# One decoder layer on one core: the first 256-column product behind 512-column products, done as two of 128 columns

## Chip, core and metric

The kernel runs on one core of a Trainium2 chip. The metric is the device time of one launch, in microseconds (us). TensorE is called PE (its weight loads PEld), VectorE DVE, ScalarE ACT, GpSimd POOL, and SyncE, which issues the weight DMAs, SP.

## What is computed

One layer on 256 tokens of width 2048: a half-step SwiGLU feed-forward (FFN), a mixer of sparse attention and a recurrent branch, and a second FFN, each followed by a layer norm. Nearly all of the arithmetic is in matrix products with weights that are read once.

```python
def swiglu(h, w_in, w_out):
    a, b = jnp.split(h @ w_in, 2, axis=-1)
    return (jax.nn.silu(a) * b) @ w_out

h = layer_norm(DN_ALPHA * h + 0.5 * swiglu(h, ffn1_w_in[l], ffn1_w_out[l]), ln1_g[l], ln1_b[l])
q, k, v, qi, ki, wi, rx, rg, gates = split_cols(h @ w_in[l])
...
y_attn = dsa_attention(q, k, v, qi, ki, wi)
y_rnn = rglru_branch(rx, rg, conv_w[l], conv_b[l], lru_wa[l], lru_ba[l], lru_wx[l], lru_bx[l], lru_lambda[l])
merged = g_attn * (y_attn @ w_attn_branch[l]) + g_rnn * (y_rnn @ w_rnn_branch[l])
h = layer_norm(DN_ALPHA * h + merged @ w_out[l], ln2_g[l], ln2_b[l])
h = layer_norm(DN_ALPHA * h + 0.5 * swiglu(h, ffn2_w_in[l], ffn2_w_out[l]), ln3_g[l], ln3_b[l])
```

## The kernel before

**Precision.** Every operand is split into two fp32r parts, a high half h and the rest l (ACT copies h, line 275; DVE subtracts to get l, line 276; the tile is `hl`). A product of two operands is three PE products: x_h·w_h, x_h·w_l, x_l·w_h. `three` (lines 743 to 745) issues these. The stationary operand is the activation (128 tokens), the moving one is the weight, and each product has its own weight load on PEld, also where two in a row have the same stationary operand.

**Two widths.** A weight piece is used either plainly, in products of 512 columns, once for each half of the tokens (`tokens`; pieces "c" of an input matrix and "o" of the FFN's output matrix), or in one of four *forms*, p1q3, p2, q5p7 and q4p6. The forms are a seven-product scheme for a 2x2 block of tokens and columns; their products have 256 columns. p2 has one operand, that is six products, and the others two, that is twelve. `blockF` runs a list of pieces (a plan), and its inner function `run` issues the products of a form. In the FFNs' main blocks (blocks 6 to 21 of 22) a plan holds 16 forms (four chunks of four) with four fills "o" among them, three ahead of the forms and one in the middle; in the other projections one or two chunks of forms alternate with plain pieces, or all are plain.

**What the forms cost elsewhere.** A form's weights are sums of weight blocks. For a chunk, DVE makes the sum tile `ws` (line 230, S below), the l part for p1q3 (`hl<-rf`), a further sum (line 234, A), the l part for p2, another sum in place (line 237, B), the l part for q5p7 (`hl<-ws`) and the l part for q4p6 (`hl<-rf`). ACT makes an h part ahead of each l part. A plain piece needs one h and one l part (`hl<-raw`), or none on DVE where its l part comes by an adding DMA (`wd`).

**Order.** PE, SP and POOL run in the order in which the program is written. DVE and ACT are ordered by the framework's scheduler, from the times that it assumes for all engines' instructions. `Weights.unit` loads and splits pieces some four ahead of PE; the ring of `hl` tiles holds five. At the end of an FFN block, `gate` combines the forms' results on DVE and ACT (tile `z`), and some pieces later PE transposes the result (four 128-column products) for the output matrix.

Of the kernel before, what the change touches and what calls it, by code (L numbers as in the profile page):

```python
# [16 lines left out]
S = 256  # L17
# [350 lines left out]
def tile_layer(ctx, tc, x_fm, x_tm, pos, f1a, f1o, wA, wki, wB, wG, lru, wab, wrb, wo, f2a, f2o,  # L368
# [6 lines left out]
    V, A, T, G = nc.vector, nc.scalar, nc.tensor, nc.gpsimd  # L375
    count = [0]

    def name(s):
        count[0] += 1
        return f"{s}{count[0]}"  # L380

    def U(s="u", dt=F32):
        return pool.tile([P, 512], dt, name=name(s), tag="u", bufs=U_BUFS)

    def UHL(s):
        return U(s, F32R).rearrange("p (a t) -> p a t", a=2)
# [10 lines left out]
    def MM():  # L397
        return psum.tile([P, 512], F32, name=name("mm"), tag="mm", bufs=4)

    def BP():  # L400
        return psum.tile([P, 512], F32, name=name("bp"), tag="bp", bufs=4)
# [60 lines left out]
    for i in range(NR + LAG):  # L462
# [4 lines left out]
        if i >= LAG:  # L467
            g, c = divmod(i - LAG, TPG)
# [17 lines left out]
    W = Weights(nc, pool, pieces, bg.paced)  # L486
# [6 lines left out]
    def share(which):  # L493

        shared.close()
        p = shared.enter_context(tc.tile_pool(name=name(which), bufs=1))
        lane[0] = p if which == "t" else None
        W.third = p if which == "s" else None
# [243 lines left out]
    def three(ps, xh, xl, w, start, stop):  # L742
        T.matmul(ps, xh, w[0], start=start, stop=False)  # L743
        T.matmul(ps, xh, w[1], start=False, stop=False)  # L744
        T.matmul(ps, xl, w[0], start=False, stop=stop)  # L745

    def tokens(ps, x, t, w, start, stop):
        three(ps, x[:, 0, t * P:(t + 1) * P], x[:, 1, t * P:(t + 1) * P], w, start, stop)

    def eager(hs, ps):  # L750
# [28 lines left out]
    def blockF(x, forms, plan, fill):  # L779

        c = e = None
        first, last = {}, {}
        for i, (f, k) in enumerate(plan):
            for b in BANKS.get(f, ()):
                first.setdefault(b, i)
                last[b] = i
        skip = 0
        if getattr(x, "halves", None):  # L790
            c = [MM(), MM()]
            eager(x, c)
            skip = 4
        for i, (form, k) in enumerate(plan):
            if i < skip:
                continue
            if form == "o":
                fill()
                continue
            if not c:  # L800
                c = [MM(), MM()]
            start, stop = ([f.get(b) == i for b in range(4)] for f in (first, last))
            if form == "c":
                for j in (k, k + 1):
                    w = W.unit(512)
                    for t in range(2):
                        tokens(c[t], x[j], t, w, start[t] and j == k, stop[t] and j > k)
                continue
            if not e:
                e = [BP(), BP()]  # L810
            c11, c12, c21 = c[0][:, :S], c[0][:, S:], c[1][:, :S]
            p1, p6, p7, q5 = e[0][:, :S], e[0][:, S:], e[1][:, :S], e[1][:, S:]
            fs = [forms[2 * k + r] for r in range(2)]

            def xop(i, t):
                return [tuple(x[4 * k + 2 * r + i][:, a, t * P:(t + 1) * P] for a in range(2)) for r in range(2)]

            def sop(i):
                return [tuple(v[:, i * P:(i + 1) * P] for v in fs[r]) for r in range(2)]

            def run(ps, ops, start, stop):
                for r in range(2):
                    three(ps, *ops[r], W.unit(S), start and r == 0, stop and r == 1)

            if form == "p1q3":
                run(p1, xop(0, 0), start[2], stop[2])
                run(c12, sop(3), start[0], stop[0])
            elif form == "p2":
                run(c11, xop(1, 0), start[0], stop[0])
            elif form == "q5p7":  # L830
                run(q5, sop(0), start[3], False)
                run(p7, sop(2), False, stop[3])
            else:
                run(c21, xop(1, 1), start[1], stop[1])
                run(p6, sop(1), start[2], stop[2])
        return c, e

    def blockA(x, finish=None, lag=0, ln=None):
# [6 lines left out]
        def half(t, k, w):  # L845
            tokens(ps[t], x[k], t, w, k == 0, k == n - 1)
# [30 lines left out]
    def split(dst, f):  # L877
        split.last = A.activation(dst[:, 0], f, AF.Copy)
        V.tensor_tensor(dst[:, 1], f, dst[:, 0], op=OP.subtract)
# [3 lines left out]
    def new_stats(widths=(24, 24)):  # L883
        stats["st"] = [SM(30, "st")[:, :n] for n in widths]
# [239 lines left out]
    def ffn(x, forms, ln):  # L1124
        def gate(c, e, g, i, lag, plain):

            z = W.fast_pool.tile([P, 4 * S], F32, name=name("z"), tag="z", bufs=Z_BUFS)
            z4 = z.rearrange("p (j c) -> p j c", j=4)
            a, b = z4[:, 0:4:2], z4[:, 1:4:2]
            if e:  # L1130
                p1, p6, p7, q5 = e[0][:, :S], e[0][:, S:], e[1][:, :S], e[1][:, S:]
                A.activation(z4[:, 0], p1, AF.Copy)
                V.tensor_tensor(z4[:, 1], z4[:, 0], p6, op=OP.add)
                V.tensor_tensor(z4[:, 2], z4[:, 1], p7, op=OP.add)
                V.tensor_tensor(b, q5[:, None, :].to_broadcast([P, 2, S]), z4[:, 1:3], op=OP.subtract)
                for t in range(2):
                    w = 512 if plain or t == 0 else S
                    zt = z[:, t * 512:t * 512 + w]
                    V.tensor_tensor(zt, zt, c[t][:, :w], op=OP.add)  # L1139
                A.activation(a, a, AF.Silu)  # L1140
            else:
                for t in range(2):
                    A.activation(z4[:, 2 * t], c[t][:, :S], AF.Silu)
                    A.activation(z4[:, 2 * t + 1], c[t][:, S:], AF.Copy)
            V.tensor_tensor(a, a, b, op=OP.mult)
            for _ in range(lag):
                yield
            ps = BP()
            for k in range(2):
                for t in range(2):  # L1150
                    T.transpose(ps[:, k * S + t * P:k * S + (t + 1) * P], z[:, t * 512 + k * P:t * 512 + (k + 1) * P], ident)
            with tc.high_priority() if lag == LAG_T[1] else nullcontext():
                for k in range(2):
                    hl = UHL("g")
                    split(hl, ps[:, k * S:(k + 1) * S])
                    g[i + k] = hl

        g = [[None] * (2 * (b1 - b0)) for b0, b1 in SEGS]
        fills = iter(FILLS)
        open_ps = []  # L1160
        acc = sums[ln.last]

        def fill():
            s, nb, k0 = next(fills)
            if k0 == 0:
                open_ps[:] = MM(), MM()
            for k in (k0, k0 + 1):
                w = W.unit(512)
                for t in range(2):
                    tokens(open_ps[t], g[s][k], t, w, k == 0, k == len(g[s]) - 1)  # L1170
            if k0 + 2 == len(g[s]):
                for t in range(2):
                    u = W.fast_pool.tile([P, 512], F32, name=name("yd"), tag="yd", bufs=2)
                    A.activation(u, open_ps[t], AF.Copy, scale=0.5)
                    G.dma_start(acc[t][nb], u, accum_op=OP.add)

        for s, (b0, b1) in enumerate(SEGS):
            for n in range(b0, b1):
                c, e = blockF(x, forms, PLANS[n], fill)
                task = gate(c, e, g[s], 2 * (n - b0), LAG_T[n == NBK - 1], ("c", 0) in PLANS[n])  # L1180
                with tc.high_priority():
                    next(task)
                bg.add("gate", task)
        def back():
            for nb in range(4):
                for t in range(2):
                    Y[t][nb] = U("y")
                    G.dma_start(Y[t][nb], acc[t][nb])
                    yield

        bg.add("back", back())
        new_stats((24, 30) if ln.last else (24, 24))
        if not ln.last:
            share("t")
            bg.add("main", later(consts(), W.last.ins))
        out_product(g[-1], ln, pair=True)
# [329 lines left out]
    for j in range(-1, NR + LAG):  # L1526
# [15 lines left out]
        if j >= LAG:  # L1542
            i = j - LAG
            g, c = divmod(i, TPG)
            xg = xcs[g * TPG:(g + 1) * TPG] if c else None
            if c == 1:
                open_heads = [BP() for _ in range(4)]
                ws = [W.unit(P) for _ in range(2)]
                for m in range(2):
                    for wi_, xi in ((0, 0), (0, 1), (1, 0)):  # L1550
                        for b in range(4):
                            rows = slice(b * TAIL, (b + 1) * TAIL)
                            T.matmul(open_heads[b][:, m * S:(m + 1) * S], ws[m][wi_][rows], xg[0][rows, xi],
                                     start=m == 0 and wi_ == 0 and xi == 0, stop=False)
            if c:
                ps = open_heads[c - 1]
# [3 lines left out]
            if c == TPG - 1:  # L1560
                ps = MM()
# [134 lines left out]
```

## Time and profile before

| | us |
|---|---|
| median of 3 runs | 2339.99 (2338.28 to 2340.84) |
| profiled execution, its own time | 2340.27 |
| its span in the trace | 2338.4 |
| PE busy in the span | 2312.5 |
| DVE busy in the span | 2201.5 |
| ACT busy in the span | 1560.0 |

The page gives busy time of each engine over the whole span. PE is busy nearly everywhere, but its busy time counts a product as busy from its start to its modelled end, so that products which follow one another at a longer distance still look like a full engine: the distance from start to start has to be read from the timeline. The granted clock of PE is 1.00 in all the stretches shown below.

### The profile page before, as it was taken

To read this page: it belongs to the slowest core of one execution; us is meant where nothing else is said; L and a number is where in the kernel's file an instruction comes from. 1 tells how busy PE (TensorE), PEld (TensorE's weight loads), DVE (VectorE), ACT (ScalarE), POOL (GpSimd) and SP (SyncE) were. 2 spreads that over 40 slices of the span, in tenths; PEclk is the share of its full clock that TensorE was granted. 3 is DMA by queue.
4 is the path that set the end of the run, shared out by engine and by line. 5 is a ranking of instruction groups with operands and counts; after the bars stand their busy time and mean duration, and the time that the engine had idled before them with its cause. 6 is when DMAs were issued, how large, how long until landed. Compare 5 with 4: busy or idle time off the path is not lost.

```text
span 2338.4 us, 40427 instructions
## 1 busy us (share of the span) xinstructions
PE 2312.5 (99%) x15430; PEld 2109.4 (90%) x15430; DVE 2201.5 (94%) x3196; ACT 1560.0 (67%) x2273; POOL 263.4 (11%) x368
## 2 busy tenths in 40 slices
PE   9999999999999999999999999999999999999998
PEld 7899999999988999888899998888889999999997
DVE  7999999999999999979887888998999999999997
ACT  7667777777757656556557785555667777777763
POOL 1101111111110000000100001100111111111111
PEclk9999999999999999999999999999999999999999
DMA  9878988888876556554675658655788888888875
GB/s 336 251 238 240 261 250 251 250 256 250 230 244 209 192 187 216 185 189 154 244 239 193 200 182 326 239 198 195 242 275 232 253 255 252 243 252 267 244 221 215
DMA packets 142178, 546.97 MB, mean 234 GB/s; under 512 B 16640, under 2 KB 17280, under 8 KB 117536
## 3 DMA queue, kind: packets, MB, share of 16 engines
q1 hardware_dynamic: 100800, 455.00, 55.1%
q0 software_dynamic: 41040, 89.27, 18.4%
q8 instruction: 120, 1.97, 0.3%
q14 instruction: 74, 0.61, 0.1%
q10 hardware_dynamic: 144, 0.13, 0.0%
HBM read 507.10 MB, written 37.22 MB: 233 GB/s over the span
## 4 chain that ended last, share of the span: by engine, by line
PE 66%; DVE 23%; issue 5%; DMA 3%; ACT 2%; POOL 0%; SPq 0%; ACTq 0%; DVEq 0%; POOLq 0%
PE mm L743 13%; PE mm L745 13%; PE mm L744 13%; DVE hl L276 13%; PE bp L744 5%; PE bp L745 5%; PE bp L743 4%; PE mm L1390 3%; PE mm L1389 3%; PE mm L1391 3%; DVE ws L230 2%; DVE rf L237 2%; DVE rf L234 2%; ACT hl L275 2%; DMA raw<-f1o 1%
## 5 line engine op out<-in xcount | busy, mean ns | idle before, releaser
L275 ACT ACTIVATE hl<-rf 128x1024 fp32r<-128x1024 f32 x573 | 511.3, 912 | 232.9 <-DVE rf L237 119.7
L276 DVE TENSOR_TENSOR hl<-rf,hl 128x1024 fp32r<-128x1024 f32 x573 | 596.9, 1047 | 8.2 <-ACT hl L275 3.8
L276 DVE TENSOR_TENSOR hl<-raw,hl 128x1024 fp32r<-128x1024 f32 (+3 forms) x402 | 474.2, 1196 | 62.2 <-ACT hl L275 61.4
L275 ACT ACTIVATE hl<-raw 128x1024 fp32r<-128x1024 f32 (+3 forms) x402 | 408.4, 1035 | 179.4 <-PE mm L745 82.8
L744 PE MATMUL bp<-hl,sh 128*128 128x256 f32 x1146 | 323.6, 282 | 10.1 <-DVE hl L276 10.1
L743 PE MATMUL bp<-hl,sh 128*128 128x256 f32 x1146 | 320.9, 280 | 0.0
L745 PE MATMUL bp<-hl,sl 128*128 128x256 f32 x1146 | 320.2, 279 | 0.0
L743 PE MATMUL mm<-hl,hs 128*128 128x512 f32 (+1 forms) x800 | 274.5, 343 | 1.6 <-DVE z L1139 0.7
L275 ACT ACTIVATE hl<-ws 128x1024 fp32r<-128x1024 f32 x191 | 202.0, 1058 | 102.7 <-DVE ws L230 71.5
L744 PE MATMUL mm<-hl,hs 128*128 128x512 f32 (+1 forms) x800 | 268.3, 335 | 0.0
L745 PE MATMUL mm<-hl,hs 128*128 128x512 f32 (+1 forms) x800 | 267.9, 335 | 0.1
L230 DVE TENSOR_TENSOR ws<-rf 128x1024 f32<-128x1024 f32 x191 | 233.8, 1224 | 5.4 <-DMA rf<-wrb 1.3
L276 DVE TENSOR_TENSOR hl<-ws,hl 128x1024 fp32r<-128x1024 f32 x191 | 234.2, 1226 | 1.8 <-ACT hl L275 1.7
L744 PEld LDWEIGHTS bp<-hl,sh 128*128 128x128 f32 x1146 | 215.4, 188 | 17.5 <-DVE hl L276 16.3
L745 PEld LDWEIGHTS bp<-hl,sl 128*128 128x128 f32 x1146 | 217.7, 190 | 0.0
L743 PEld LDWEIGHTS bp<-hl,sh 128*128 128x128 f32 x1146 | 215.4, 188 | 1.3
L1389 PE MATMUL mm<-hs,hl 128*128 128x256 f32 x640 | 178.3, 279 | 0.0
L1391 PE MATMUL mm<-hs,hl 128*128 128x256 f32 x640 | 177.8, 278 | 0.0
L1390 PE MATMUL mm<-hs,hl 128*128 128x256 f32 x640 | 177.7, 278 | 0.0
L743 PEld LDWEIGHTS mm<-hl,hs 128*128 128x128 f32 x800 | 150.4, 188 | 19.1 <-issue 2.6
L745 PEld LDWEIGHTS mm<-hl,hs 128*128 128x128 f32 x800 | 151.0, 189 | 16.7 <-DVE hs L937 0.5
L744 PEld LDWEIGHTS mm<-hl,hs 128*128 128x128 f32 x800 | 150.5, 188 | 14.3 <-DVE hl L276 0.2
(360 smaller groups left out, 5897.6 us busy)
## 6 DMA issues: line engine op xcount, KB each, us to landing
rf<-f1a SPq DMA_DIRECT2D x75, 1024.0 KB, 7.7
rf<-f2a SPq DMA_DIRECT2D x75, 1024.0 KB, 7.5
raw<-f1o SPq DMA_DIRECT2D x88, 512.0 KB, 6.6
raw<-f2o SPq DMA_DIRECT2D x88, 512.0 KB, 6.6
raw<-wB SPq DMA_DIRECT2D x80, 512.0 KB, 4.8
raw<-wG SPq DMA_DIRECT2D x54, 512.0 KB, 4.2
ya<-yd POOLq DMA_DIRECT2D x80, 256.0 KB, 7.4
rf<-wA SPq DMA_DIRECT2D x20, 1024.0 KB, 5.5
```

Of the source, the lines that this page charges most:

```text
L230: v.tensor_tensor(t, b[:, 0:4:3], b[:, 1:2].to_broadcast([P, 2, 2, 256]), op=OP.add)
L234: v.tensor_tensor(b[:, 1], t[:, 1], b[:, 0], op=OP.add)
L237: v.tensor_tensor(b[:, 0], b[:, 1], b[:, 2], op=OP.add)
L275: nc.scalar.activation(hp, src, AF.Copy)
L276: self.last = nc.vector.tensor_tensor(lp, src, hp, op=OP.subtract)
L743: T.matmul(ps, xh, w[0], start=start, stop=False)
L744: T.matmul(ps, xh, w[1], start=False, stop=False)
L745: T.matmul(ps, xl, w[0], start=False, stop=stop)
L1389: T.matmul(ps[:, :S], w[0], x[:, 0], start=first, stop=False)
L1390: T.matmul(ps[:, :S], w[0], x[:, 1], start=False, stop=False)
L1391: T.matmul(ps[:, :S], w[1], x[:, 0], start=False, stop=last)
```

## The change

A flag, `after_wide`, is set by every 512-column `tokens` call, and cleared when a gate's transposes are issued or when a form's run has used it. Where it is set, the first operand of the form is done by `entry` in place of `three`: the x_h·w_h product of 256 columns becomes two products of 128 columns on the two halves of the same PSUM tile and the same weights' halves. The other two products stay as they are. That is one product and one weight load more at each such place.

```diff
+    after_wide = [False]
+
+    def entry(ps, xh, xl, w, start, stop):
+        n = w[0].shape[1] // 2
+        for c in range(2):
+            T.matmul(ps[:, c * n:(c + 1) * n], xh, w[0][:, c * n:(c + 1) * n], start=start and c == 0, stop=False)
+        T.matmul(ps, xh, w[1], start=False, stop=False)
+        T.matmul(ps, xl, w[0], start=False, stop=stop)
+
     def tokens(ps, x, t, w, start, stop):
+        after_wide[0] = w[0].shape[1] == 512
         three(ps, x[:, 0, t * P:(t + 1) * P], x[:, 1, t * P:(t + 1) * P], w, start, stop)
...
             def run(ps, ops, start, stop):
                 for r in range(2):
-                    three(ps, *ops[r], W.unit(S), start and r == 0, stop and r == 1)
+                    w = W.unit(S)
+                    (entry if after_wide[0] else three)(ps, *ops[r], w, start and r == 0, stop and r == 1)
+                    after_wide[0] = False
...
             ps = BP()
+            after_wide[0] = False
             for k in range(2):
                 for t in range(2):
                     T.transpose(ps[:, k * S + t * P:k * S + (t + 1) * P], z[:, t * 512 + k * P:t * 512 + (k + 1) * P], ident)
```

On PE, in the first FFN: behind the last 512-column product of a piece, the first product of a form's operand (`sh`, `sl` are the activation's h and l parts).

```order
 L744 MATMUL mm_635<-hl_611,xs_150 128x512
 L745 MATMUL mm_635<-hl_611,xs_150 128x512
-L743 MATMUL bp_655<-hl_638,sh_315 128x256
-L744 MATMUL bp_655<-hl_638,sh_315 128x256
-L745 MATMUL bp_655<-hl_638,sl_316 128x256
+L752 MATMUL bp_655<-hl_638,sh_315 128x128 x2
+L753 MATMUL bp_655<-hl_638,sh_315 128x256
+L754 MATMUL bp_655<-hl_638,sl_316 128x256
 L743 MATMUL bp_655<-hl_638,sh_341 128x256
```

One product became two; this is so at 154 places of the program, and nothing else moved on PE, SP or POOL.

DVE's rows did move, in each of the FFNs' main blocks. Before, on DVE, at the end of the third chunk and in the fourth:

```order
L237 TENSOR_TENSOR rf_4308<-rf_4308 128x2x256
L276 TENSOR_TENSOR hl_4415<-ws_4379,hl_4415 128x1024
L230 TENSOR_TENSOR ws_4455<-rf_4376 128x1024
L276 TENSOR_TENSOR hl_4431<-rf_4308,hl_4431 128x1024
L276 TENSOR_TENSOR hl_4454<-rf_4376,hl_4454 128x1024
L234 TENSOR_TENSOR rf_4376<-ws_4455,rf_4376 128x2x256
```

The same place of the changed kernel:

```order
L237 TENSOR_TENSOR rf_4334<-rf_4334 128x2x256
L276 TENSOR_TENSOR hl_4441<-ws_4405,hl_4441 128x1024
L276 TENSOR_TENSOR hl_4457<-rf_4334,hl_4457 128x1024
L230 TENSOR_TENSOR ws_4481<-rf_4402 128x1024
L276 TENSOR_TENSOR hl_4480<-rf_4402,hl_4480 128x1024
L234 TENSOR_TENSOR rf_4402<-ws_4481,rf_4402 128x2x256
```

The sum S of the next chunk (line 230) moved behind the l part of q4p6, which now follows the l part of q5p7 directly.

Before, on DVE, from the end of a block's first chunk through its second:

```order
L276 TENSOR_TENSOR hl_4626<-rf_4501,hl_4626 128x1024
L230 TENSOR_TENSOR ws_4646<-rf_4564 128x1024
L276 TENSOR_TENSOR hl_4645<-rf_4564,hl_4645 128x1024
L234 TENSOR_TENSOR rf_4564<-ws_4646,rf_4564 128x2x256
L276 TENSOR_TENSOR hl_4664<-rf_4564,hl_4664 128x512
L237 TENSOR_TENSOR rf_4564<-rf_4564 128x2x256
L276 TENSOR_TENSOR hl_4676<-ws_4646,hl_4676 128x1024
L879 TENSOR_TENSOR g_4700<-bp_4695,g_4700 128x256
L276 TENSOR_TENSOR hl_4692<-rf_4564,hl_4692 128x1024
```

The same place of the changed kernel:

```order
L276 TENSOR_TENSOR hl_4653<-rf_4528,hl_4653 128x1024
L230 TENSOR_TENSOR ws_4673<-rf_4591 128x1024
L234 TENSOR_TENSOR rf_4591<-ws_4673,rf_4591 128x2x256
L276 TENSOR_TENSOR hl_4672<-rf_4591,hl_4672 128x1024
L276 TENSOR_TENSOR hl_4692<-rf_4591,hl_4692 128x512
L237 TENSOR_TENSOR rf_4591<-rf_4591 128x2x256
L276 TENSOR_TENSOR hl_4704<-ws_4673,hl_4704 128x1024
L230 TENSOR_TENSOR ws_4761<-rf_4690 128x1024
L276 TENSOR_TENSOR hl_4720<-rf_4591,hl_4720 128x1024
```

The sum A (line 234) now follows S, whose result it reads, directly, and the third chunk's S now follows the l part of q5p7, which reads the tile that this S writes over. ACT's rows moved in the same blocks, mainly two copies of the middle fill's result (`yd`) behind the h parts of the fourth chunk's p1q3.

## Rows read from the trace of the kernel before

**Rows 1.** The page's first part: busy us, share of the span, instructions.

```profile
PE 2312.5 (99%) x15430; PEld 2109.4 (90%) x15430; DVE 2201.5 (94%) x3196; ACT 1560.0 (67%) x2273; POOL 263.4 (11%) x368
```

**Rows 2.** Windows of FFN blocks: stretch, us, busy by engine (instructions), PE clock, DMA.

```profile
1780.00:2280.00 500.00, 495.54 (x3509) 462.22 (x3508) 498.33 (x607) 358.38 (x502) 83.90 (x97) 1.00 0.83 247
...
249.76:281.49 31.73, 31.17 (x220) 29.07 (x220) 31.39 (x38) 22.83 (x33) 5.33 (x6) 1.00 0.89 252
281.49:312.90 31.41, 31.13 (x221) 29.04 (x221) 31.30 (x38) 22.72 (x33) 5.33 (x6) 1.00 0.86 249
```

**Rows 3.** The same view of three stretches in the mixer.

```profile
1144.00:1201.00 57.00, 57.00 (x363) 51.83 (x362) 55.77 (x66) 33.07 (x36) 4.97 (x10) 1.00 0.63 222
1433.00:1534.00 101.00, 101.00 (x575) 88.82 (x574) 95.38 (x127) 53.71 (x65) 16.35 (x31) 1.00 0.76 270
...
886.00:951.00 65.00, 65.00 (x514) 63.03 (x514) 64.68 (x100) 39.54 (x47) 1.08 (x2) 1.00 0.55 197
```

**Rows 4.** PE's timeline, 30 products behind 512-column ones: start, us, tiles, columns.

```profile
638.25 0.28 PE L743 MATMUL bp<-hl,xs 128*128 128x256 f32 x1
...
641.79 0.60 PE L1151 MATMUL bp<-ident,z 128*128 128x128 f32 x4
```

**Rows 5.** PE's timeline behind those transposes, and into the next 512-column products.

```profile
642.34 0.28 PE L744 MATMUL mm<-hl,xs 128*128 128x256 f32 x1
...
642.92 0.28 PE L743 MATMUL bp<-hl,sh 128*128 128x256 f32 x1
...
648.36 0.39 PE L743 MATMUL mm<-wd,g 128*128 128x512 f32 x1
...
649.29 0.39 PE L744 MATMUL mm<-wd,g 128*128 128x512 f32 x1
```

**Rows 6.** PEld's timeline where PE had stood idle for a weight part.

```profile
249.76 0.19 PEld L744 LDWEIGHTS bp<-hl,sh 128*128 128x128 f32 x1 [0.45 <-DVE hl L276]
249.87 0.19 PEld L745 LDWEIGHTS bp<-hl,sl 128*128 128x128 f32 x1
```

**Rows 7.** PE's timeline behind another such wait: the first and last of 22 distances.

```profile
1904.00 0.28 PE L745 MATMUL bp<-hl,sl 128*128 128x256 f32 x1
...
1906.60 0.40 PE L743 MATMUL mm<-hl,g 128*128 128x512 f32 x1
```

**Rows 8.** DVE's timeline in one FFN block: line 230 twice, and three parts.

```profile
2017.59 1.23 DVE L230 TENSOR_TENSOR ws<-rf 128x1024 f32<-128x1024 f32 x1
2018.72 1.23 DVE L276 TENSOR_TENSOR hl<-rf,hl 128x1024 fp32r<-128x1024 f32 x1
...
2021.66 1.23 DVE L276 TENSOR_TENSOR hl<-ws,hl 128x1024 fp32r<-128x1024 f32 x1
2022.92 1.23 DVE L230 TENSOR_TENSOR ws<-rf 128x1024 f32<-128x1024 f32 x1
...
2028.14 1.22 DVE L276 TENSOR_TENSOR hl<-ws,hl 128x1024 fp32r<-128x1024 f32 x1
2029.44 1.22 DVE L276 TENSOR_TENSOR hl<-rf,hl 128x1024 fp32r<-128x1024 f32 x1
```

**Rows 9.** DVE's timeline in the mixer: line 230 with line 234 directly behind it.

```profile
914.45 1.22 DVE L230 TENSOR_TENSOR ws<-rf 128x1024 f32<-128x1024 f32 x1
915.70 0.69 DVE L234 TENSOR_TENSOR rf<-ws,rf 128x512 f32<-128x512 f32 x1
```

**Rows 10.** ACT's timeline in an FFN block: parts and copies one behind the other.

```profile
2019.62 1.05 ACT L275 ACTIVATE hl<-ws 128x1024 fp32r<-128x1024 f32 x1
2020.57 1.14 ACT L182 ACTIVATE wd<-raw 128x512 fp32r<-128x512 f32 x2
2021.61 0.58 ACT L1174 ACTIVATE yd<-mm 128x512 f32<-128x512 f32 x1
2022.09 1.05 ACT L275 ACTIVATE hl<-rf 128x1024 fp32r<-128x1024 f32 x1
```

## The prediction

> **What bounds the kernel now.** I read the page's busy times first [rows 1]: PE 99% of the span, DVE 94%. That names two candidates, so the next view is the busy time by stage, and there the kernel falls into two kinds of stretch. In the FFNs' main blocks DVE is the full engine: 498.33 of 500 us, against 495.54 for PE [rows 2]. A block takes 31.41 us, of which DVE is busy 31.30; in the block ahead of it DVE's rows were delayed by 0.3 us and the block took 31.73 [rows 2], so a gap on DVE lengthens the block one for one. PE has slack there: once in each block it stands 0.2 to 0.5 us, waiting for a weight part from DVE (two such waits stand ahead of [rows 6, 7]). In most of the mixer it is the other way: PE is busy 57.00 of 57.00 and 101.00 of 101.00 us while DVE has gaps; in 886 to 951 us both are nearly full, DVE 64.68 of 65 [rows 3].
>
> The third view is PE's timeline, from start to start. The 30 products of 256 columns behind 512-column ones start every (641.79 - 638.25) / 30 = 0.118 us [rows 4]. Behind four 128-column transposes the pace changes: five distances of 0.116 on average, then 48 of (648.36 - 642.92) / 48 = 0.1133 [rows 5]. So PE has two paces for the same products, 0.0046 us apart (0.1179 over the first 29 distances of rows 4, less 0.1133), and in the trace it keeps the slow one behind 512-column products until something interrupts it. The change puts two 128-column products at this point.
>
> **The change on PE.** The first price is the pair itself. Each product has its own weight load. Where PE had stood empty, two loads in a row started 0.11 us apart [rows 6], twice the 0.0567 us that 128 columns would need at half of 0.1133. The first of the pair has its load hidden behind the 512-column product before it; the second waits 0.11 for its load, and the next product again: 0.22 to 0.23 in place of 0.118. So a pair costs **+0.11** at each place. The bounds are 0 (both loads hidden, two streams of 0.0567) and +0.118 (each half as long as a slow product); I take the value of the load row, the nearest.
>
> TensorE: Matmul & The Clock Gate, a page of the Trainium skill, gives in its section on the back-to-back issue gap N/2.4 + 2.5 ns for a product of N columns, 56 ns for 128. By it a pair takes 112 ns, no more than the product that it replaces, and this term would be nothing. The load row (0.11 us) speaks against it; it is the second rival.
>
> The second price is what the pace gives back. I take it that the pair brings the fast pace, as the transposes do [rows 5]: both make PE's pace depend on weight loads for a moment. Against it: the transposes are four, of another kind, and a wait for a weight part, which also empties PE, did not always do so (22 distances of 0.118 behind it [rows 7]). If it comes, a run of n products gives back 0.0046 n, less 0.013 for settling (five distances, 0.58 against 0.567 [rows 5]) and 0.02 for the first four 512-column products behind a fast run (0.93 for four [rows 5], against 0.907 for eight times 0.1133). Net: 0.145 - 0.0046 n, where plain pieces follow: +0.09 for n = 12, +0.06 for 18, +0.035 for 24, even at 31, and a gain beyond.
>
> Of the 154 places (counted in the order), 81 lie in the FFNs' DVE-bound blocks, where neither sign reaches the end: a block's two pairs are 0.22 on an engine with 0.2 to 0.5 us of slack. The other 73 are on PE's own path:
> - the first FFN's first blocks (5 runs of 12 and 18): +0.4
> - early mixer (7 runs, 12 to 30): +0.3
> - 824 to 954 us (9 runs, four of 90, two of 66): -1.5 on PE, of which DVE, full in 64.68 of 65 [rows 3], lets perhaps -0.5 through
> - attention and behind it (12 runs, eight of them 8 to 20 long behind other small products, some already fast and then paying the whole 0.11): +0.9
> - 1144 to 1201 us and the recurrent branch's start (6 of 18, 5 of 24, one of 216): +0.4 + 0.2 - 0.9 = -0.3
> - 1433 to 1535 us (4 of 18, 14 of 12, 2 of 6): +1.8
> - the last projection (4 of 18, 4 of 24): +0.4
>
> Sum **+3.0**.
>
> **The change on DVE.** The order shows that the scheduler has put DVE's rows of the FFN blocks in another order. The work is the same, but more rows stand directly behind the row on which they depend. The trace prices that. Line 230 followed by independent work takes 1.13 us to the next start (2017.59 to 2018.72), and so does a 1024-column part [rows 8]. The l part of q5p7 followed by S, which overwrites its input, takes 1.26: +0.13 [rows 8]. The same part followed by the l part of q4p6, which waits for ACT's h part, which waits for B, takes 1.30: +0.17 [rows 8]. S followed by A, which reads it, takes 1.25: +0.12 [rows 9]. Counting these neighbours in the two orders, over the DVE rows of 151 to 651 us and from 1764 us to the end of the second FFN: S, A 0 before and 31 now; l part then S 28 and 33; l part then q4p6 36 and 63. That is 31 x 0.12 + 5 x 0.13 + 27 x 0.17 = 3.7 + 0.65 + 4.6 = **+9.0**, or 0.28 in each of 32 blocks, nothing of it hidden while DVE is the full engine. PE can't become the bound through it: 31.41 less its wait, plus 0.22, is under 31.69.
>
> VectorE: DVE Perf Modes, in the Trainium skill, says under "The DRAIN you can't avoid" that a DVE instruction waits for the pipeline to empty in any case, and measured a chain of copies as equally long with and without a semaphore behind each. By it a dependent neighbour costs nothing and the +9.0 would be 0. Rows 8 and 9 (1.26 and 1.25 against 1.13) disagree for this kernel; it is the third rival.
>
> ACT moved too. In the fourth chunk of a block its new order runs, behind B of the third, h of q4p6, h of p1q3, then two `yd` and four `wd` copies mixed with h of p2, and only then h of q5p7. With steps of 0.95, 0.48 and 0.52 [rows 10] that part is ready 0.12 + 2 x 0.95 + 2 x 0.48 + 5 x 0.52 + 1.06 = 6.6 us behind B's end, some 0.2 us later than DVE could start its l part by the steps of rows 8; the 0.17 which this place costs anyway is then spent already. That leaves 0 to 0.06 a block, 0 to 2 us; I take **+1**. Not lower than 0 but for 0.6 us: two of the blocks before had such a lateness of 0.3.
>
> **The sum** is made on the profiled execution: span 2338.4, with 1.9 around it 2340.27. 2340.27 + 3.0 + 9.0 + 1.0 = 2353.3. The median of the three runs is 0.28 lower: **2353**.
>
> **The rivals.**
> 1. *The pair doesn't bring the fast pace* (the change doesn't do what it says). For it: rows 7, and the 30 slow products of rows 4, which no start irregularity ends. Then each of the 73 places costs 0.11: 73 x 0.11 = 8.0 in place of 3.0: 2358. Chance 0.25.
> 2. *The pair is free*, and the pace turns fast: 73 x 0.11 less, 3.0 - 8.0 = -5.0, with DVE's 10: 2345. Against it: rows 6. Chance 0.09.
> 3. *DVE's new order costs nothing*, because what I price as a dependence is hidden in the blocks, or the chip's own order of arrival differs: only PE's +3.0 is left, 2343. Against it: the steps of rows 8 and 9 and a block that grew by its DVE gap [rows 2]. Chance 0.09.
> 4. *Not slower: the FFN blocks follow PE, not DVE.* If the 31.41 us came from PE's release of the five `hl` tiles to ACT, DVE's new gaps would be filled in the slack, and the fast pace would pay in each block: the 30 products before the transposes even out (0.125 - 0.138), the 60 behind the middle fill give 0.276 less 0.125, together 0.16 a block, 32 x 0.16 = 5 us, less 3.0: 2338. It decides as soon as DVE's gaps in a block are waits for PE; 31.30 busy of 31.41 [rows 2] leaves 0.11 for them. Chance 0.05.
>
> **How the numbers follow.** The forecast (fast pace, DVE's order priced by its rows) has 0.52, and its own range is 2349 to 2356 (ACT 0 to 2, PE's terms by 2). The range reaches up over most of the first rival and down to the second, 2345 to 2359; the third, the fourth and the tails are left out. About 0.2%, 4.7 us, is what a measurement of this kernel can tell from no change, that is 2335.3 to 2344.7. Faster by more needs the fourth rival with a free pair: 0.03. Within: most of the third and fourth, half of the second: 0.14. Slower: 0.83.
>
> **What would show it.** Step one: two 128-column products of line 752 with 0.11 us from the first to the second and 0.11 to the next; 0.06 would be the second rival. Step two: starts 0.113 apart behind them, 0.118 for the first rival. Step three: an FFN block of 31.7 us in place of 31.41, with line 234 1.25 behind line 230; an unchanged 31.41 would be the third rival, a shorter one the fourth. The stretch of 1433 to 1534 us should grow by 1.8 us (2.2 without the fast pace). The prediction is wrong if the blocks keep their length, or if DVE's gaps there have another size than the few rows that price them.

## The result: 2360.15 us in place of 2339.14, and where it went

| | before | after |
|---|---|---|
| median of 4 runs (us) | 2339.14 (2337.77 to 2340.84) | 2360.15 (2359.79 to 2361.80) |
| ratio, 95% interval | 1 | 1.0090 (1.0074 to 1.0106) |
| span of the profiled execution | 2338.4 | 2360.0 |

Slower by 21.0 us, where +13 was forecast: the sign is right, and the time lies above the upper end of the range, 2359. The page's first part of the changed kernel answers to [rows 1]; PE and DVE stay the two full engines:

```profile
PE 2322.9 (98%) x15584; PEld 2110.0 (89%) x15584; DVE 2209.2 (94%) x3196; ACT 1554.3 (66%) x2273; POOL 265.7 (11%) x368
```

To see where the 21 us arise I laid the two PE timelines side by side, product by product (a pair counted as one product), and read by how much the changed kernel lags. The lag grows by 0.6 us up to the FFN blocks, 5.9 over the first FFN's main blocks, **3.7 at that FFN's end**, 2.0 in the mixer, 6.2 over the second FFN's main blocks and **2.7 at its end**; 0.2 us that it starts ahead make up the rest of the 21.0 at the last product (another 0.6 of the span stands behind that product). So there are three causes, of 2.6 (the pair, with what the mixer adds), 12.1 and 6.5 us. The first two were forecast as 3 and 10, the third not at all.

**The pair.** PE's timeline at one of the places (columns as in [rows 4]):

```profile
1448.38 0.39 PE L745 MATMUL mm<-hl,yr 128*128 128x512 f32 x1
1448.61 0.33 PE L752 MATMUL bp<-hl,sh 128*128 128x128 f32 x2
1448.78 0.33 PE L753 MATMUL bp<-hl,sh 128*128 128x256 f32 x1
1448.95 0.28 PE L754 MATMUL bp<-hl,sl 128*128 128x256 f32 x1
...
1450.09 0.39 PE L743 MATMUL mm<-hl,yr 128*128 128x512 f32 x1
```

The two products of the pair take 0.17 us together (the second starts 0.06 behind the first, at 1448.67) and the product behind them another 0.17. That is 0.34 where two products at the slow pace [rows 4] took 0.236: the pair costs 0.10 to 0.11. From line 754 on, ten distances take 1.14 us, 0.114 each: the pace is the fast one of [rows 5].

**The FFN block.** Its window (columns as in [rows 2]):

```profile
540.24:572.07 31.83, 31.30 (x224) 28.93 (x224) 31.52 (x39) 22.66 (x33) 5.30 (x6) 1.00 0.86 253
```

31.83 us in place of 31.41, in 28 of the 32 blocks alike within 0.01. DVE's timeline of this block (columns as in [rows 8]; in brackets the idle time ahead of a row and what ended it) shows what it is made of:

```profile
550.58 1.22 DVE L230 TENSOR_TENSOR ws<-rf 128x1024 f32<-128x1024 f32 x1
551.83 0.69 DVE L234 TENSOR_TENSOR rf<-ws,rf 128x512 f32<-128x512 f32 x1
...
554.78 1.22 DVE L276 TENSOR_TENSOR hl<-ws,hl 128x1024 fp32r<-128x1024 f32 x1
556.03 1.23 DVE L230 TENSOR_TENSOR ws<-rf 128x1024 f32<-128x1024 f32 x1
...
558.31 0.42 DVE L891 TENSOR_TENSOR g<-bp,g 128x256 fp32r<-128x256 f32 x1
...
561.32 0.68 DVE L237 TENSOR_TENSOR rf<-rf 128x512 f32<-128x512 f32 x1
562.21 1.23 DVE L276 TENSOR_TENSOR hl<-ws,hl 128x1024 fp32r<-128x1024 f32 x1 [0.21 <-ACT hl L275]
...
567.97 0.69 DVE L237 TENSOR_TENSOR rf<-rf 128x512 f32<-128x512 f32 x1
568.68 1.23 DVE L276 TENSOR_TENSOR hl<-ws,hl 128x1024 fp32r<-128x1024 f32 x1
569.86 1.23 DVE L276 TENSOR_TENSOR hl<-rf,hl 128x1024 fp32r<-128x1024 f32 x1
```

An undisturbed step is 1.135 us for 1024 columns and 0.60 for 512. Above that stand: S to A 0.117 (1.25), the l part of q5p7 to S 0.117 (1.25), B to the third chunk's l part of q5p7 0.295 (0.89), B to the fourth chunk's 0.11 (0.71) and from there to the l part of q4p6 0.04: 0.68 us in a block. Before it was 0.29: 0.13 and 0.16, the two steps of [rows 8]. The difference, 0.39, is nearly the whole of the 0.42 by which the block grew, so gaps on DVE lengthen it one for one.

The 0.295 is a wait for ACT. ACT's timeline there (columns as in [rows 10]):

```profile
558.76 0.38 ACT L890 ACTIVATE g<-bp 128x256 fp32r<-128x256 f32 x1 [0.99 <-DVE g L891]
559.04 1.14 ACT L182 ACTIVATE wd<-raw 128x512 fp32r<-128x512 f32 x2
...
561.13 1.05 ACT L275 ACTIVATE hl<-ws 128x1024 fp32r<-128x1024 f32 x1
...
567.59 1.05 ACT L275 ACTIVATE hl<-ws 128x1024 fp32r<-128x1024 f32 x1
```

ACT's second g copy waits for DVE's first g row (558.31), which now stands behind S and an l part; four `wd` copies stand behind that copy, and the h part for the third chunk's q5p7 behind those. From there ACT is busy without a break to the fourth chunk's h part, 567.59 + 1.05.

**The FFN's end.** PE's timeline, ACT's and POOL's DMA issues at the end of the first FFN:

```profile
675.88 0.39 PE L745 MATMUL mm<-hl,g 128*128 128x512 f32 x1
678.66 0.47 PE L743 MATMUL mm<-hl,g 128*128 128x512 f32 x1 [2.39 <-DVE z L1151]
...
679.98 0.63 PE L744 MATMUL mm<-hl,g 128*128 128x512 f32 x1
680.41 0.63 PE L745 MATMUL mm<-hl,g 128*128 128x512 f32 x1
```
```profile
674.85 1.06 ACT L275 ACTIVATE hl<-raw 128x1024 fp32r<-128x1024 f32 x1 [5.60 <-DMA raw<-f1o]
```
```profile
660.40 0.87 POOL L1188 DMA_DIRECT2D ya<-yd  x1 [26.87 <-ACT yd L1187]
661.58 0.88 POOL L1188 DMA_DIRECT2D ya<-yd  x1 [0.30 <-issue]
662.12 4.11 POOL L1201 DMA_DIRECT2D y<-ya  x7
```

The same of the kernel before, where PE does not stand still there:

```profile
665.55 1.06 ACT L275 ACTIVATE hl<-raw 128x1024 fp32r<-128x1024 f32 x1 [2.72 <-DMA raw<-f1o]
```
```profile
651.51 0.88 POOL L1175 DMA_DIRECT2D ya<-yd  x1 [25.68 <-ACT yd L1174]
653.71 0.87 POOL L1175 DMA_DIRECT2D ya<-yd  x1 [1.32 <-ACT hl L275]
654.25 4.11 POOL L1188 DMA_DIRECT2D y<-ya  x7
```

The changed kernel lags 6.3 us at this place. The transfers that add `yd` start 8.9 and 7.9 later, so 2.6 and 1.6 later than the lag alone, the loads of y behind them 1.6; and ACT then waits 5.60 us, not 2.72, for a raw piece, whose load lands 7.2 us behind its issue, where it took 4.3 before. The piece's l part comes late on DVE, with z rows of the gate queued behind it; PE stands 2.39 us until a z row has freed a PSUM tile. After this idle time PE runs at half clock for some 3 us: 0.43 a 512-column product, not 0.227, in this window (columns as in [rows 2]):

```profile
680.00:682.00 2.00, 2.00 (x6) 1.61 (x5) 2.00 (x6) 1.46 (x2) 0.00 (x0) 0.50 0.50 147
```

### The profile page after: what moved, and what is told of

It reads as the page before. It is cut to its first block, busy times and chain, and to the rows that moved or that the text cites. A ratio compares the mean times of both kernels' runs of the same rounds, so it can differ in the third digit from the quotient of the medians.

```text
span 2360.0 us, 40660 instructions
## 1 busy us (share of the span) xinstructions
PE 2322.9 (98%) x15584; PEld 2110.0 (89%) x15584; DVE 2209.2 (94%) x3196; ACT 1554.3 (66%) x2273; POOL 265.7 (11%) x368
## 4 chain that ended last, share of the span: by engine, by line
PE 48%; DVE 33%; ACT 9%; issue 8%; DMA 2%; POOL 0%; SPq 0%; DVEq 0%; ACTq 0%; POOLq 0%
DVE hl L276 17%; PE mm L743 10%; PE mm L744 10%; PE mm L745 10%; DVE ws L230 5%; ACT hl L275 4%; PE mm L1404 3%; PE mm L1402 3%; PE mm L1403 3%; DVE rf L234 2%; DVE rf L237 2%; PE bp L743 2%; PE bp L744 2%; PE bp L745 2%; ACT wd L185 2%
## 5 line engine op out<-in xcount | busy, mean ns | idle before, releaser
L744 PE MATMUL bp<-hl,sh 128*128 128x256 f32 x1113 | 311.3, 280 | 5.9 <-DVE hl L276 5.9
L743 PE MATMUL bp<-hl,sh 128*128 128x256 f32 x1113 | 308.0, 277 | 0.0
L745 PE MATMUL bp<-hl,sl 128*128 128x256 f32 x1113 | 307.7, 276 | 0.0
L744 PEld LDWEIGHTS bp<-hl,sh 128*128 128x128 f32 x1113 | 209.0, 188 | 12.1 <-DVE hl L276 11.8
L743 PEld LDWEIGHTS bp<-hl,sh 128*128 128x128 f32 x1113 | 209.1, 188 | 0.1
L745 PEld LDWEIGHTS bp<-hl,sl 128*128 128x128 f32 x1113 | 209.0, 188 | 0.0
L744 PE MATMUL mm<-hl,g 128*128 128x512 f32 (+1 forms) x408 | 162.4, 398 | 9.4 <-DVE hl L276 9.4
L743 PEld LDWEIGHTS mm<-hl,hs 128*128 128x128 f32 x797 | 149.8, 188 | 20.0 <-ACT yd L1187 3.2
L745 PEld LDWEIGHTS mm<-hl,hs 128*128 128x128 f32 x797 | 149.7, 188 | 16.7 <-DVE hs L949 0.5
```

## The experiments

Eleven kernels were run, in groups that share the runs of the kernel before (medians 2340.1, 2340.0 and 2340.3). In most of them DVE's and ACT's rows are held in a given order by edges between neighbours, which add no instruction:

```diff
+        for a, b in zip(order[LO:HI], order[LO + 1:HI]):
+            tc.add_manual_dep(mine[b], mine[a].name, mybir.DependencyInfo(
+                mybir.DependencyClass.NoSync, mybir.DependencyReason.DATA), reason="order")
```

`order` is the order of DVE's (or ACT's) rows of some kernel, `mine` the rows as the program writes them. In the diffs of orders below S, A and B are lines 230, 234 and 237, `hf` the 1024-column part of p1q3 or q4p6, `hf2` that of p2, `hw` that of q5p7, `hr` that of a plain piece; `g`, `z`, `wd`, `yd` as before.

**Does holding an order cost anything?** The changed kernel, held in its own order.

> The changed kernel with its own order of DVE's and ACT's rows pinned: the same instructions in the same order. Pinning costs nothing: 2360 us within 1.5, FFN blocks of 31.83 us, stalls at the FFNs' ends. If pinning itself changed the time, all kernels with pinned rows would have to be read against this one.

2361.3 us (2359.95 to 2362.53), 1.0086 (1.0069 to 1.0103); blocks of 31.83, stalls at both ends (the lag grows by 3.7 and 4.7 us there). That is 1.1 us above the changed kernel's median, with runs that overlap: holding an order costs nothing that these runs can tell, and the second profile of this order shows the same three causes.

**Products or order?** First the changed kernel's products with the order of before, then the reverse.

> PE does the products of the changed kernel (pairs at all 154 places); DVE's and ACT's rows are pinned, row by row, to the order of the kernel before. Theory A (the time went into the order of DVE's and ACT's rows): only PE's term is left. Between the traces of before and after, PE's lag outside the FFNs grows by 0.4 (first blocks) and by 2.3 to 2.7 (mixer); so 2339.1 + 2.5 = 2341.6 us, FFN main blocks of 31.41 us, no stall at the FFNs' ends. Rival B (PE's pairs and its faster pace lengthen the FFN blocks themselves, whatever the order): blocks stay near 31.83 and the time near 2358 to 2360 us.

2342.8 us, 1.0011 (1.0001 to 1.0020). A block's window (PE 31.13, DVE 31.30 of 31.41, as in [rows 2]):

```profile
471.53:502.94 31.41, 31.13 (x225) 29.03 (x224) 31.30 (x40) 22.82 (x33) 5.33 (x6) 1.00 0.86 249
```

> PE does the products of the kernel before (no pair anywhere); DVE's and ACT's rows are pinned, row by row, to the order of the changed kernel. Theory A: FFN main blocks of 31.83 us (12.1 us in all), a stall at the end of each FFN (3.7 and 2.7 us), nothing in the mixer: 2339.1 + 18.5 = 2357.6 us. Rival B: blocks of 31.41 us and 2339 to 2341 us. If blocks and ends are longer only where pair and order come together, the time is between.

2358.8 us, 1.0078 (1.0063 to 1.0093), without a single pair; a block's window:

```profile
507.52:539.34 31.82, 31.46 (x223) 29.07 (x222) 31.52 (x39) 22.65 (x33) 5.30 (x6) 1.00 0.84 247
```

Theory A holds in both directions, against 2340.1 for the kernel before in the same group: the order alone costs 18.7 us (18.5 expected), the products alone 2.7 (2.5 expected), and their sum, 21.4, is about the change's 21.0.

The totals agree better than their parts, and that is in part luck. In the profile of the order alone the two ends add 1.5 and 3.8 us, not 3.7 and 2.7, and the mixer adds 1.0, not nothing: DVE's and ACT's rows moved in the mixer too, and not only in the FFNs' main blocks (of the 876 places at which DVE's two orders differ, 198 lie from 700 to 1700 us). In the profile of the products alone, which is the slowest of its ten runs, PE lags 5.5 us at the end: 3.3 come from the mixer, and 1.6 from two short waits for `g` rows at the second FFN's end, where no stall was expected. So the two totals and the 12.1 us of the blocks are shown; how the rest divides between mixer and ends differs from profile to profile.

**Which of the block's gaps?** Three edits of the changed kernel's order.

```diff
 hf S
-A hf
+hf A
 hf2 B
```

> The changed kernel, its own order pinned, but in the 30 FFN blocks the second chunk's A stands behind the l part of p1q3, not directly behind S. Theory P (a row directly behind the one that it reads costs DVE 0.117, and DVE is the full engine): blocks of 31.83 - 0.117 = 31.71 us, 2360.2 - 3.5 = 2356.7 us. Rival Q (the next wait for ACT takes up what is saved, since ACT's part comes when it comes): the wait of 0.295 in the third chunk grows to 0.41, blocks stay at 31.83, 2360 us.

2357.7 us, 1.0077 (1.0062 to 1.0092), 2.5 less than the changed kernel (3.6 less than that kernel held in its own order); blocks of 31.70. The 0.117 behind S is gone, the other gaps are as they were: theory P.

Next, S behind g on DVE; and, in another kernel, ACT's four wd copies out of the way:

```diff
 B hw
-S hf g
+hf g S
 hf g A
```

> The changed kernel, its own order pinned, but in every FFN main block the third chunk's S stands behind the l part of q4p6 and the first g row, where it stood ahead of both. Theory F (S ahead of g makes DVE's g row 1.13 us later, so ACT's second g copy and the four wd copies behind it, so that ACT's h part for the third chunk's q5p7 is 0.295 us late): that wait goes, and the step from the l part of q5p7 to S (0.117); the l part of q4p6 may now wait up to 0.157 for its h part. Blocks 31.83 - 0.255 to 0.41 = 31.42 to 31.57 us, 2360.2 - 8 to 13 = 2347 to 2352 us. Rival G (ACT is late for its own amount of work, not for S): the wait stays, only 0.117 goes: 31.71 us and 2356.5 us.

```diff
 g
-wd wd wd wd hw
+hw wd wd wd wd
```

> The changed kernel, its own order pinned, but in the 30 FFN blocks that have them ACT's four wd copies stand behind the h part for the third chunk's q5p7, ahead of which they stood. Theory F: the part is ready in time and DVE's wait of 0.295 goes: blocks of 31.54 us, 2360.2 - 30 x 0.295 = 2351.3 us. Rival G: ACT has 2.1 us more to do behind it, so the wait only moves to the fourth chunk's parts (0.15 there today): blocks of 31.8 us and 2359 to 2360 us.

2363.7 us, 1.0102 (1.0087 to 1.0117), and 2361.0, 1.0093 (1.0078 to 1.0108): no gain in either, and blocks of 31.82 and 31.78. DVE's timeline of the first:

```profile
552.48 1.22 DVE L276 TENSOR_TENSOR hl<-ws,hl 128x1024 fp32r<-128x1024 f32 x1
553.78 1.23 DVE L276 TENSOR_TENSOR hl<-rf,hl 128x1024 fp32r<-128x1024 f32 x1
...
559.06 0.68 DVE L237 TENSOR_TENSOR rf<-rf 128x512 f32<-128x512 f32 x1
559.66 1.22 DVE L276 TENSOR_TENSOR hl<-ws,hl 128x1024 fp32r<-128x1024 f32 x1
560.95 1.23 DVE L276 TENSOR_TENSOR hl<-rf,hl 128x1024 fp32r<-128x1024 f32 x1
...
565.57 0.68 DVE L237 TENSOR_TENSOR rf<-rf 128x512 f32<-128x512 f32 x1
566.41 1.23 DVE L276 TENSOR_TENSOR hl<-ws,hl 128x1024 fp32r<-128x1024 f32 x1 [0.16 <-ACT hl L275]
```

Theory F was half right. The 0.295 is gone in both kernels (559.06 + 0.60 is 559.66, no gap), so S ahead of g and the four copies do cause it. But the next step, to the l part of q4p6, now waits 0.157 (1.29), as it did not while its predecessor was late, and the fourth chunk's l part waits 0.246 instead of 0.11, since ACT's chain behind the third B (two h parts, two yd, four wd, two h parts) is as long as it was. In the first kernel the same 0.157 also took the place of the 0.117 to S. The waits are three places of one chain between DVE and ACT: taking the first away uncovers the next. For the wd copies rival G is right about the time (2359 to 2360); for S behind g neither theory is (2347 to 2352 and 2356.5).

**ACT's order without DVE's.** The products and DVE's order of before, ACT's order of the changed kernel. (The reverse, DVE's new order with ACT's old one, wasn't tried; I take it that their rows would wait for each other in a circle, which no run shows.)

> The products of the kernel before and DVE's rows in the order of before; only ACT's rows are pinned to the order of the changed kernel. Theory F2 (ACT's new order costs only where DVE's comes with it: with S behind both g rows, ACT's second g copy is early, and only the chain of 6.7 us behind the third chunk's B is left, which makes the fourth chunk's l part 0.11 late and takes up the 0.157 that stood behind it): blocks of 31.40 to 31.45 us; the yd copies of the last block are late as in the changed kernel, so the stalls at the FFNs' ends stay, 2 to 5 us: 2342 to 2346 us. Rival G2 (ACT's order alone makes the blocks longer): 31.6 us or more, 2350 us or more.

2395.7 us, 1.0238 (1.0223 to 1.0253): theory F2 is far off, and rival G2 (31.6 us or more) has the sign but not the size. Blocks take 32.9 us, and DVE's timeline shows new waits:

```profile
524.84 0.69 DVE L1145 TENSOR_TENSOR z<-z 128x512 f32<-128x512 f32 x1 [0.60 <-ACT z L1140]
...
532.22 0.42 DVE L879 TENSOR_TENSOR g<-bp,g 128x256 fp32r<-128x256 f32 x1 [0.34 <-ACT g L878]
...
545.14 1.22 DVE L276 TENSOR_TENSOR hl<-ws,hl 128x1024 fp32r<-128x1024 f32 x1 [0.18 <-ACT hl L275]
```

I had looked at the parts alone. ACT's new order also has an h part ahead of the z and g copies for which DVE's old order asks first; that part waits for B, and DVE waits with it. The two orders belong together, so their 18.7 us can't be divided between the engines.

**The ends.** Two edits of the changed kernel's order, in the last main block of each FFN: ACT's yd copies back where they were, and DVE's next three z rows ahead of the l part that waits.

```diff
 g hw
-hf hf yd yd
+yd hf yd hf
 hf2
```

> The changed kernel with its own order pinned, but in the last main block of each FFN ACT's two yd copies stand where they stood before: one ahead of the h part for q4p6, the other ahead of the h part for p1q3. Theory C (the stall at the FFN's end is a late load: the yd copies come later, so their accumulating transfers and the loads of y that wait for those come later, and run beside the load of the fifth raw piece, which lands 7.3 us behind its issue where it was 4.3): both stalls go, 2360.2 - 6.4 = 2353.8 us, at least 4 us less. Rival D (the place of yd is no cause; the stall is DVE's order, z rows queued behind an l part that waits): within 1 us of 2360.

2358.3 us, 1.0078 (1.0063 to 1.0093). The profile shows the mechanism as theory C has it: transfers earlier, the raw piece's load 4.9 us from issue to landing in place of 7.2, a wait of 3.31 in place of 5.60, at the first FFN's end no stall of PE and a clock of 1.00:

```profile
658.54 0.87 POOL L1188 DMA_DIRECT2D ya<-yd  x1 [24.97 <-ACT yd L1187]
...
661.19 4.64 POOL L1201 DMA_DIRECT2D y<-ya  x8
```
```profile
673.07 1.06 ACT L275 ACTIVATE hl<-raw 128x1024 fp32r<-128x1024 f32 x1 [3.31 <-DMA raw<-f1o]
```

The ends add 0.3 and 0.9 us of lag in place of 3.7 and 2.7. Over seven profiles, ACT's longest wait for a raw piece there is 2.7 to 4.3 us with early yd copies (before, old order, this one; both FFNs) and 4.5 to 6.1 with late ones (changed, held in its own order, new order alone, the next one); the other four kernels with the late copies (A behind the l part, S behind g, the wd copies moved, ACT's order alone) lie between, at 5.2 to 6.0. But the median fell by 2 to 3 us, not by the 6.4 expected. In this kernel's profile the mixer, with the same rows, took 4 us longer than in the changed kernel's (lag 6.1 against 2.0), most of it in 1201 to 1433 and 1534 to 1752 us. Seven profiles with these products and this order of the mixer's rows add anything from 2 to 6 us there. Why is open; so the ends' share of the median is only bounded, from 2 to some 6 us.

```diff
-hr z z z
+z z z hr
```

> The changed kernel with its own order pinned, but at the end of each FFN DVE's next three z rows stand ahead of the l part of the fifth raw piece, which they followed. Theory C: that piece lands as late as in the changed kernel, PE then waits for it alone, about 1 us in place of 2.4, and the clock may still fall: 2360.2 - 3 = 2357 us (2356 to 2358.5). Rival D (the z rows behind the waiting part are the whole of it): no stall, 2353.8 us.

2358.6 us, 1.0076 (1.0061 to 1.0091). ACT waits as long as in the changed kernel (5.67 and 5.86), and the stall shrinks at the first FFN's end (lag 1.0 in place of 3.7) but not at the second's (3.9), where PE now waits later and for other rows. Rival D (2353.8) falls; theory C (2357) is nearer. The z rows behind the part are a part of the stall; its source is the late piece, as the edit of the yd copies showed.

**Gaps taken away altogether.** The kernel before, without pairs, with a second tile for S's result, paid for by two U tiles.

```diff
-U_BUFS = 53
+U_BUFS = 51
-WS_BUFS = 1
+WS_BUFS = 2
```

> The kernel before, without any pair, with two ws tiles in place of one (and two U tiles fewer, to make room): S no longer writes over the tile that the l part of q5p7 reads, and the scheduler makes an order of its own, in which no S follows that l part and no A follows its S directly. Theory P: the 0.275 us of such steps in a block shrink to 0.15 or less, and the block to between 31.3 and PE's 31.13 plus its wait, say 31.2: 2339.1 - 32 x 0.2 = 2332.7 us (2331 to 2337). Rival R (the blocks follow PE or ACT, not these steps): 31.4 us and 2339 us. If the two U tiles are missed in the mixer, it grows there.

2347.9 us, 1.0035 (1.0022 to 1.0047), slower; but the FFN blocks are 31.12 us and the first FFN gains 6.9. The scheduler's order also changed in the mixer, which lost 8.6 us in 954 to 1205 and 5.3 in 1433 to 1535. So the mixer was held in the order of before:

> Two ws tiles without any pair, as in the kernel with two ws tiles, but between the FFNs DVE's and ACT's rows are pinned to the order of the kernel before, since the mixer lost 8 and 5 us there with the scheduler's new order (954 to 1205 us, 1433 to 1535 us). Theory P: FFN blocks of 31.12 us, the mixer as before: 2340 - 32 x 0.28 = 2331 us (2329 to 2334), faster than both kernels. Rival T (the mixer's loss came from the two U tiles given up): the mixer loses 8 us or more again, 2339 us or more.

**2331.4 us** (2330.3 to 2332.3), 0.9960 (0.9945 to 0.9975): faster than both kernels. The mixer is back (rival T falls, it was the order there too), blocks take 31.12 us, and DVE has hardly a gap left. A stretch of 31.20 us in which PE and DVE are both busy throughout, and the two rows of [rows 8] that stood 1.26 apart:

```profile
530.00:561.20 31.20, 31.20 (x223) 29.13 (x222) 31.20 (x39) 22.98 (x33) 5.34 (x6) 1.00 0.87 254
```
```profile
1918.84 1.22 DVE L276 TENSOR_TENSOR hl<-ws,hl 128x1024 fp32r<-128x1024 f32 x1
1919.98 1.22 DVE L230 TENSOR_TENSOR ws<-rf 128x1024 f32<-128x1024 f32 x1
```

The same two lines in the same order stand 1.14 apart when S writes another tile. The l parts of q5p7 and q4p6 mostly have another row between them now; where they still meet in the FFNs, in 11 places, they stand 1.14 apart in all but one.

## Why the prediction was right in sign and too low

- **What bounds the kernel: right.** DVE in the FFNs, one for one: 0.39 us more of gaps, 0.42 more in a block. The fourth rival falls with it: with the order of before the pairs leave the block at 31.41.
- **The pair's price, +0.11, and the fast pace: right** (0.10 to 0.11; 0.114 behind it). The first and the second rival fall. The sign that I named for it was not: the second 128-column product starts 0.06 behind the first, which I had named as the sign of the second rival, and the pair is still not free. The next product starts 0.11 behind it, and the one after that another 0.17, which pays the rest. The formula by which the prediction makes a pair 112 ns is, in the section on the back-to-back issue gap of TensorE: Matmul & The Clock Gate, of the Trainium skill, the gap of an isolated product. In this stream the pair takes 0.17 us.
- **PE's sum, +3.0: right as far as it can be told**: 2.7 by the medians of the old order with pairs (0.2 to 4.7 by the interval; its one profile lags 5.5). By stretch, forecast and measured in the changed kernel: the early mixer +0.3 and -0.1; 824 to 954 us -0.5 and -0.55; 1144 to 1433 -0.3 and -0.14; 1433 to 1534 +1.8 and +1.55. That last stretch also grows by 1.55 with the old order and by 0.00 with the new order alone. Attention is less clear: it grows by 0.8 with pairs alone, by 1.1 with the order alone and by 1.05 with both.
- **DVE's order, +9.0 and ACT's +1: right kind, too small**: 12.1 in the blocks. S to A (0.117 for 0.12) was sized rightly, as the edit of A alone showed. The step that failed is "l part then q4p6, 27 x 0.17": there the l part of q5p7 is itself late by 0.295, behind ACT, and in the fourth chunk by 0.11. I counted neighbours and gave each a price from one row. I did ask for ACT's lateness, but in the fourth chunk alone, where "6.6 us behind B's end" was right to 0.1 us; in the third chunk I did not follow S ahead of g to ACT's second g copy, and from there through four wd copies.
- **The ends: the step that is missing.** I had named the two yd copies that moved and priced them as rows of ACT. Each has a transfer behind it, and the loads of y wait for those. In the blocks inside an FFN no lag of theirs shows; behind the last one they meet the loads of the next raw pieces. The forecast put this at nothing. It is 6.5 us in one profile, 8.4 in another of the same order and 5.3 with the order alone; what the medians give back without it, 2 to 3, leaves its exact size open. With the 2 us of the blocks it is what the forecast lacked.
- **The third rival** (the order is free) falls most plainly: 18.7 us for the order alone. By the Trainium skill, VectorE: DVE Perf Modes, section "The DRAIN you can't avoid", a chain of copies took the same time with a semaphore behind each and with one behind the last. No run here times that; but what the prediction took from it, that a dependent neighbour costs nothing, the rows contradict: the same neighbours stand 1.14 us apart in the last kernel, where nothing is shared, and 1.25 in the changed one, where the second writes over what the first reads.

## What to carry to other kernels

Where a scheduler orders engines by its own clock, an edit on one engine is an edit of the order on the others: hold the order still when the edit is to be measured, and read the moved rows as part of the edit. Gaps between rows of two engines that wait for each other can't be priced or taken away one by one; follow the chain from row to row, and expect that removing one wait uncovers the next. A copy that moves takes its transfers along, and the place to look is the last round of a loop, where other transfers start.

## What the runs showed of the hardware

- DVE's A directly behind S, whose result it reads, and S directly behind the l part whose input it writes over, start 1.249 to 1.258 us after the row ahead in the FFNs of the changed kernel, where unrelated rows start 1.135 after one of this size: 0.114 to 0.123 us more (0.12 to 0.14 for the second kind in the trace of the kernel before). It is gone for A when another row stands between them, and for S when it writes another tile (1.134 to 1.138 in 33 places). Whether the engine itself or the wait that stands between the two rows costs it, no run separates.
- Behind the stall of 2.39 us at the first FFN's end the granted clock fell to 0.50, its lower level of 1.2 GHz, for some 3 us, which cost seven products 0.2 us each. Behind one of 2.45 us at the second FFN's end it stayed at 1.00, and no run shows what tells the two apart:

```profile
2313.00:2315.00 2.00, 2.00 (x10) 1.61 (x10) 2.00 (x3) 2.00 (x3) 0.00 (x0) 1.00 0.45 160
```
